# A hybrid SSD and gated-delta layer on one core: every engine's order taken from a list schedule over a first build

## The chip, the cores and the metric

The kernel runs on one core of a Trainium2 chip. The core has five engines that run their own instruction streams in order and wait for one another by semaphores: TensorE (PE in the profile, its weight loads PEld), VectorE (DVE), ScalarE (ACT), GpSimd (POOL) and SyncE (SP), which here issues nearly all DMA transfers. The metric is the device time of one execution in microseconds (us). The kernel before takes 2354.13 us in the median of three runs (2348.30 to 2360.07).

## The reference

One layer of width 2048 over 1024 latent tokens with a context of 256 tokens ahead of them:

```python
mod_lat = silu(c) @ w_ada + b_ada;  mod_ctx = silu(c_ctx) @ w_ada + b_ada      # shift, scale, gate
u_l = rms_norm(x, pre_w) * (1 + scale_l) + shift_l                             # u_c alike from ctx
z, xbc, dt, qkv, b, a = split_proj(u @ w_in)
xbc = silu(conv5(xbc) + bias);  qkv = silu(conv5(qkv))
y = ssd_scan in both directions (16 heads of 64, state 128, chunks of 128), the context's state first
o = gdn_scan in both directions (8 heads of 128, chunks of 128):
    v_new = u_i - w_i @ S;  o_i = q_i @ S + attn_i @ v_new;  S = S * dec + k_i^T @ v_new
    (u_i, w_i solve a unit triangular 128 x 128 system per chunk)
yo = concat(ssd_out_norm(y, z), gdn_out_norm(o, z))
out = x + gate_l * rms_norm(yo @ w_out, post_w)                                # latent tokens only
```

All is float32; the kernel makes each product of the large projections from two float16 parts of either factor (three matmuls per block).

## The kernel before, in words

Tokens stand in 10 chunks of 128 (8 latent, 2 context), channels on partitions. The program is one class, `Layer`; `build()` walks a list of steps. In order of time: `start` and the modulation (w_ada, w_in and x loaded; 0 to 200 us), `gates()` (step sizes and decays of all heads; its last vector result is `la`, L570, which L579 and L591 to L593 bring into the cumulative sums), the first GDN projections with `gate_rows()` (the gate's columns of w_ada in sixteen loads of 1 MB, three buffers `x`, matmuls L325), then eight GDN heads, four SSD quarters, and the output projection (L1138).

A GDN head `h` has these parts. `gdn_prep` makes for each chunk the product of k with itself (L693) and with q (L695), and the decayed matrices A (L697) with `gb`, whose decays come by DMA (L686). `invert_blocks` inverts the diagonal 32 x 32 blocks of all twenty matrices: four transposes (L715), a store to DRAM (L716, L717), a load of X (L721), and 30 times a pair of DVE operations, L726 and L728, each of which needs the one before. `gdn_chain` runs ten steps in each of two directions, d = 0 and 1; a step is PE L850 and L852 (state S with k and q), DVE L856 (r), PE L866 (r through the inverse), DVE L871 (xw) and ACT L873, PE L876, DVE L881 (the next S), PE L888, DVE L889 (o). Tile names carry the direction: `ps_c0`, `r1`, `S0`, `xw1`. `gdn_end` and `gdn_post` finish one head and start another. An SSD quarter runs over the ten chunks twice; in the second pass it reads the matrices E (two buffers, DMA).

Between these parts stand the projections of later blocks: `conv_block` and `z_block` load 512 KB of w_in at a time (six buffers `w`), split it in float16 parts (ACT L408 and L411, DVE L413, with a small sum on PE, L134), and `group` runs 48 matmuls (L437) into a PSUM bank; the bank is emptied by one ACT and four DVE operations (L498), and ACT L502 and DVE L503 follow. The banks are `ps_d` (two) and in the GDN heads `ps_e` (one). This is the work that fills PE while a chain waits. All order is set by the framework's own scheduler: each instruction has a priority by its place in the program, and the scheduler picks for each engine, by its own costs, the ready instruction with the best one. Semaphores are then set from the dependencies.

Of the kernel before, what the change touches and what calls it, by code (L numbers as in the profile page):

```python
# [1 line left out]

# [5 lines left out]
F32 = mybir.dt.float32  # L8
# [6 lines left out]
P = 128  # L15
DM = 2048
KB = DM // P
KH = KB // 2
NL = 1024
NC = 256  # L20
T = NL + NC
NCH = T // P
# [22 lines left out]
class Layer:  # L45


    def __init__(self, ctx, tc, a, out):
        self.ctx, self.tc, self.nc, self.a, self.out = ctx, tc, tc.nc, a, out
        self.pool = lambda name, bufs=1, **kw: ctx.enter_context(tc.tile_pool(name=name, bufs=bufs, **kw))  # L50
        self.const = self.pool("const")
        self.phase_pool = None
        self.psum = self.pool("psum", bufs=1, space=bass.MemoryType.PSUM)
        self.dram = self.pool("dram", space=bass.MemoryType.DRAM)
        self.sk = self.psum.tile([P, 512], F32, tag="s", name="ps_s", bufs=1)
        self.nd = self.nk = self.ns = 0
        self.z7 = [None, None]
# [1232 lines left out]
        self.phase_pool.close()  # L1290


@with_exitstack
def hybrid_layer_kernel(ctx, tc, a, out):
    Layer(ctx, tc, a, out).build()


_INS = ['x', 'c', 'ctx', 'c_ctx', 'w_ada', 'b_ada', 'pre_norm_w', 'post_norm_w', 'w_in', 'conv_ssd_w', 'conv_ssd_b',
        'conv_gdn_w', 'ssd_a_log', 'ssd_dt_bias', 'ssd_d', 'ssd_norm_w', 'gdn_a_log', 'gdn_dt_bias', 'gdn_norm_w',
        'w_out']  # L1300
# [19 lines left out]
```

## Time and profile before

| | before |
|---|---|
| median of 3 runs | 2354.13 us (2348.30 to 2360.07) |
| profiled execution, its own time | 2351.73 us |
| its span | 2350.0 us |
| PE busy | 2162.5 us, 92% |
| DVE busy | 1399.5 us, 60% |
| ACT busy | 998.5 us, 42% |
| mean granted clock of PE | 0.978 |

The span is the stretch from the first to the last instruction. An engine's busy time is the time in which it executed an instruction; time in which it waited for a semaphore is idle. In a table by stretches each row gives, for one stretch, the busy us of each engine with the number of instructions, then the granted clock of PE (1.00 is full speed), the busy share of the DMA engines, and GB/s. A wait reads: who waited, in which line and tile, for which engine's instruction, then the total, the number and the longest, in us. In a timeline a row is a start, a duration and an instruction (equal neighbours merged, with x and their number), and in brackets how long the engine had been idle and what released it.

### The profile page before, as it was taken

The numbers are of one execution on the slowest core, as the hardware profiler recorded it, in microseconds if no ns is written. First come the engines' busy times: TensorE is split into PE (matmuls) and PEld (weight loads), VectorE is DVE, ScalarE is ACT, GpSimd is POOL, SyncE is SP. The second block draws the span as 40 slices with busy tenths as digits, with TensorE's granted clock in tenths as the row PEclk, the third lists the DMA queues.
The fourth block names the chain that finished last, engine by engine and source line by source line (L and its number), as shares of the span: only waits on it lengthen the run. The fifth ranks groups of instructions, "written<-read, shape, count | busy, mean of one in ns | idle before, by whom it ended". The sixth has DMA issues, their size and how long they took to land. (4 is left out here: it accounts for less than half of the span.)

```text
span 2350.0 us, 41855 instructions
## 1 busy us (share of the span) xinstructions
PE 2162.5 (92%) x16070; PEld 1379.2 (59%) x16070; DVE 1399.5 (60%) x3499; ACT 998.5 (42%) x2493; POOL 268.7 (11%) x514
## 2 busy tenths in 40 slices
PE   4989999889999898998989999999999999899998
PEld 4334644456665655556555566555555555788887
DVE  5335543869694856858568486566767773511214
ACT  6026422344444352433524444465667584423320
POOL 1000001012111020111201110130303130000000
PEclk9999999999999999999999999999999999999999
DMA  9952347454444344343443444333465355212117
GB/s 323 348 164 55 80 145 217 117 131 106 134 115 120 101 126 116 88 133 93 121 119 85 127 123 115 99 90 108 111 183 149 98 164 195 68 37 73 55 37 269
DMA packets 397236, 301.71 MB, mean 128 GB/s; under 512 B 61339, under 2 KB 358684, under 8 KB 395628
## 3 DMA queue, kind: packets, MB, share of 16 engines
q1 hardware_dynamic: 386668, 293.80, 43.7%
q10 hardware_dynamic: 10368, 5.24, 0.8%
q8 instruction: 126, 2.06, 0.4%
q14 instruction: 74, 0.61, 0.1%
HBM read 241.41 MB, written 57.57 MB: 127 GB/s over the span
## 5 line engine op out<-in xcount | busy, mean ns | idle before, releaser
L437 PE MATMUL ps_d<-u,w 128*128 128x512 f16 (+1 forms) x4560 | 969.6, 357 | 8.3 <-DVE cv L498 4.6
L437 PEld LDWEIGHTS <-w 128*128 128x128 f16 x6048 | 595.3, 100 | 494.3 <-issue 36.4
L1138 PEld LDWEIGHTS <-u 128*128 128x128 f16 x3072 | 298.7, 98 | 50.9 <-DMA u<-in_w_out_dram 13.2
L437 PE MATMUL ps_e<-u,w 128*128 128x512 f16 (+1 forms) x1296 | 314.5, 376 | 0.0
L498 DVE SCALAR_TENSOR_TENSOR cv<-ps_d,taps,cv 128x496 f32<-128x496 f32 (+3 forms) x300 | 194.8, 650 | 80.0 <-ACT cv L492 38.6
L413 DVE SCALAR_TENSOR_TENSOR w<-w,scl 128x512 f16<-128x512 f32 (+1 forms) x204 | 149.9, 777 | 50.8 <-ACT w L411 50.3
L408 ACT ACTIVATE w<-w 128x1024 f16<-128x1024 f32 (+1 forms) x102 | 106.5, 1044 | 167.7 <-DMA w<-in_w_in_dram 101.5
L1138 PE MATMUL ps_d<-wx,u 128*128 128x256 f16 x1536 | 170.2, 273 | 4.6 <-DMA u<-in_w_out_dram 4.6
L1138 PE MATMUL ps_d<-w,u 128*128 128x256 f16 x1296 | 144.8, 273 | 5.7 <-DMA u<-in_w_out_dram 3.8
L1168 DVE SCALAR_TENSOR_TENSOR raw<-ps_d,inv,gp 128x256 f32<-128x256 f32 x59 | 28.4, 483 | 193.2 <-ACT jko L1166 193.2
L411 ACT ACTIVATE w<-w,scl 128x1024 f16<-128x1024 f32 (+1 forms) x102 | 112.3, 1133 | 36.2 <-DVE scl L145 16.5
L1166 ACT ACTIVATE jko<-ps_d,inv 128x256 f32<-128x256 f32 x59 | 27.8, 471 | 182.4 <-PE ps_d L1138 177.4
L989 ACT ACTIVATE E<-E,G 128x128 f32<-128x128 f32 x256 | 80.9, 388 | 35.1 <-DMA E<-gr 29.6
L690 ACT ACTIVATE gb<-gb 128x256 f32<-128x256 f32 x80 | 32.2, 413 | 147.0 <-DVE gb L676 144.0
L502 ACT ACTIVATE t<-cv 128x512 f32<-128x512 f32 (+1 forms) x98 | 55.7, 570 | 90.0 <-DVE cv L498 75.4
L676 DVE SCALAR_TENSOR_TENSOR gb<-gb,G,mneg 128x128 f32<-128x128 f32 x160 | 50.8, 345 | 69.2 <-DMA gb<-gr 67.9
L873 ACT ACTIVATE r<-ps_c,nb 128x128 f32<-128x128 f32 x128 | 45.7, 364 | 107.0 <-DVE xw L871 97.2
L876 PE MATMUL ps_c<-xw,vq 128*128 128x128 f32 x288 | 61.8, 304 | 30.8 <-DVE xw L871 14.2
L726 DVE TENSOR_TENSOR tp<-X 80x30 f32<-80x30 f32 (+14 forms) x240 | 77.6, 323 | 13.9 <-DMA X<-d 13.2
L876 PEld LDWEIGHTS ps_c<-xw,vq 128*128 128x128 f32 x288 | 47.4, 196 | 58.9 <-ACT r L873 33.7
L503 DVE SCALAR_TENSOR_TENSOR cv<-t,cv 128x512 f32<-128x512 f32 (+1 forms) x98 | 60.5, 618 | 31.7 <-ACT t L502 31.3
L728 DVE TENSOR_TENSOR X<-X,tp 80x30 f32<-80x30 f32 (+14 forms) x240 | 78.4, 327 | 0.6
(329 smaller groups left out, 3250.4 us busy)
## 6 DMA issues: line engine op xcount, KB each, us to landing
w<-in_w_in_dram SPq DMA_DIRECT2D x102, 512.0 KB
x<-in_w_ada_dram SPq DMA_DIRECT2D x48, 1024.0 KB
vq<-vq SPq DMA_DIRECT2D x128, 256.0 KB
E<-gr SPq DMA_DIRECT2D x64, 256.0 KB
u<-in_w_out_dram SPq DMA_DIRECT2D x24, 512.0 KB
gb<-gr SPq DMA_DIRECT2D x80, 128.0 KB
x<-in_x_dram SPq DMA_DIRECT2D x8, 1024.0 KB
vq<-gb SPq DMA_DIRECT2D x64, 128.0 KB
```

The costliest lines, as they stand in the source:

```text
L408: nc.scalar.activation(out=w16[h][:, 0], in_=w[h], func=AF.Square, accum_out=ssq[:, h:h + 1])
L411: nc.scalar.activation(out=w16[h][:, 0], in_=w[h], func=AF.Copy, scale=t)
L413: nc.vector.scalar_tensor_tensor(out=w16[h][:, 1, s], in0=w[h][:, s], scalar=t, in1=w16[h][:, 0, s], op0=ALU.mult, op1=ALU.subtract)
L437: self.nc.tensor.matmul(out=ps, lhsT=w16[k // KH][:, a, k % KH], rhs=self.u16[b][k][:, lo:lo + n], start=(k == 0 and i == 0), stop=(k == K ...
L498: nc.vector.scalar_tensor_tensor(out=o3[:, :, lo_o:hi_o], in0=p3[:, :, lo_o + s:hi_o + s], scalar=taps[tap], in1=o3[:, :, lo_o:hi_o], op0= ...
L502: nc.scalar.activation(out=t[:, 0:n], in_=o, func=AF.Tanh)
L503: nc.vector.scalar_tensor_tensor(out=o, in0=t[:, 0:n], scalar=1.0, in1=o, op0=ALU.add, op1=ALU.mult)
L726: nc.vector.tensor_tensor(out=t, in0=X[:, k + 1:, k:k + 1].to_broadcast(sh), in1=X[:, k:k + 1, 0:k].to_broadcast(sh), op=ALU.mult)
L728: nc.vector.tensor_tensor(out=X[:, k + 1:, 0:k], in0=X[:, k + 1:, 0:k], in1=t, op=ALU.add)
L876: nc.tensor.matmul(out=pS, lhsT=vq[:, 1], rhs=xw, start=True, stop=True)
L989: nc.scalar.activation(out=E[:, d, r], in_=E[:, d, r], func=AF.Identity, bias=self.G[:, j, c:c + 1])
L1138: self.nc.tensor.matmul(out=ps, lhsT=self.y16(k, p, s), rhs=w16[k // 4][:, q, k % 4], start=(i == 0 and j == 0), stop=(i == KB - 1 and j = ...
```

## The change

The kernel is built twice. The first build is the one before. From it the class `Plan` takes every instruction that the framework ordered, with its dependencies, buffers and priority, gives each a duration from tables by engine and size, and makes a list schedule: at each point the engine that is free earliest takes, of the instructions whose inputs are ready, the one with the best priority. Up to `fixed` = 250 us of planned time the program's own order is kept. A result reaches another engine 90 ns after its end (200 from PE), and a PE instruction is held to be ready another `lead` = 700 ns later; between dependent instructions of one engine the plan has no gap. A DMA starts 1300 ns after its issue and lands 500 ns after its last byte. Buffers count too: an instruction that reuses a place in SBUF or PSUM follows those that used it. The second build gets, for each engine, an edge from each instruction to the next of the plan (an order without a semaphore). No instruction's arithmetic changes; the second build gives its tiles to other buffers of the same pool in some places, and the number of semaphore instructions differs a little. Lines of the class stand two lower in the new file, so L866 is there L868.

```diff
+class Plan:
+    DVE_TT = ((1, 150), (128, 285), (256, 415), (512, 690))
...
+    AFTER = {"PE": 200, "SP": 0}
...
+        def issue(k, t):
+            nonlocal rate
+            e = self.engine[k]
+            free[e] = end = t + self.cost[k]
+            if self.dma[k]:
+                whole, alone = self.dma[k]
+                s = max(t + 1300, rate)
+                rate = s + max(whole, alone * .3)
+                end = s + max(whole, alone * .6) + 500
+            done[k] = True
+            if k < real:
+                self.order[e].append(self.names[k])
+            for q in after[k]:
+                gap = 0 if max(k, q) >= real or (e == self.engine[q] and not self.dma[k]) else self.AFTER.get(e, 90)
+                if gap and self.engine[q] == "PE":
+                    gap += self.lead
+                ready[q] = max(ready[q], end + gap)
+                count[q] -= 1
+                if not count[q]:
+                    heapq.heappush(will[self.engine[q]], (ready[q], self.prio[q], q))
...
+        while k < real and max(free.values()) < fixed:
...
+            issue(k, max(free[self.engine[k]], ready[k]))
+            k += 1
...
+        while not all(done):
+            best = None
+            for e in free:
+                while will[e] and will[e][0][0] <= free[e]:
+                    _, p, k = heapq.heappop(will[e])
+                    heapq.heappush(can[e], (p, k))
+                t = free[e] if can[e] else will[e][0][0] if will[e] else None
+                if t is not None and (best is None or t < best[0]):
+                    best = t, e
+            t, e = best
+            k = heapq.heappop(can[e])[-1] if can[e] else heapq.heappop(will[e])[-1]
+            issue(k, max(t, ready[k]))
...
+    def draw(self, tc, nc):
+
+        info = mybir.DependencyInfo(mybir.DependencyClass.NoSync, mybir.DependencyReason.SCHED_ONLY)
+        last = {b: a for names in self.order.values() for a, b in zip(names, names[1:])}
+        for i in nc.all_instructions():
+            if i.name in last:
+                tc.add_manual_dep(i, last[i.name], info, reason="order")
...
+    nc = build(Plan(*build(None), lead=700, fixed=250e3))[0]
```

Three places show how the order moves. The first is PE in a step of a GDN head's chain (`ps_c0_7506` and `ps_c1_7524` are the same step in the two directions; `ps_m_8344` and `ps_m_8358` hold transposes of a later head). Before:

```order
L850 MATMUL ps_c0_7506<-S0_7482,cv_4868 128x128
L852 MATMUL ps_c0_7506<-S0_7482,vq0_7484 128x128
L850 MATMUL ps_c1_7524<-S1_7500,cv_4868 128x128
L852 MATMUL ps_c1_7524<-S1_7500,vq1_7502 128x128
...
L866 MATMUL ps_c0_7506<-r0_7509,A_5681 128x128
...
L866 MATMUL ps_c1_7524<-r1_7527,A_5681 128x128
...
L876 MATMUL ps_c0_7506<-xw0_7514,vq0_7484 128x128
...
L888 MATMUL ps_c0_7506<-r0_7513,vq0_7484 128x128
L876 MATMUL ps_c1_7524<-xw1_7532,vq1_7502 128x128
```

Now:

```order
L852 MATMUL ps_c0_7506<-S0_7482,cv_4868 128x128
L854 MATMUL ps_c0_7506<-S0_7482,vq0_7484 128x128
...
L868 MATMUL ps_c0_7506<-r0_7509,A_5681 128x128
...
L852 MATMUL ps_c1_7524<-S1_7500,cv_4868 128x128
L854 MATMUL ps_c1_7524<-S1_7500,vq1_7502 128x128
...
L878 MATMUL ps_c0_7506<-xw0_7514,vq0_7484 128x128
...
L98 MATMUL ps_m_8344<-ident_138,cv_7808 128x128 x4
L98 MATMUL ps_m_8358<-ident_138,cv_7808 128x128 x4
L890 MATMUL ps_c0_7506<-r0_7513,vq0_7484 128x128
L868 MATMUL ps_c1_7524<-r1_7527,A_5681 128x128
```

The first gap holds three projection matmuls (L437) before, and the others three, one, three and none; now the gaps hold nine, one, six and sixty-one (L439), and the second direction's L868 comes after all of these.

The second place is DVE at the inversion of the next head's blocks (X_7346, tp_7347), about the same steps. Before:

```order
L726 TENSOR_TENSOR tp_7347<-X_7346 80x30
L881 SCALAR_TENSOR_TENSOR S0_7554<-S0_7518,cd_2200,ps_c0_7542 128x128
L728 TENSOR_TENSOR X_7346<-X_7346,tp_7347 80x30
L498 SCALAR_TENSOR_TENSOR cv_7808<-ps_d_7866,taps_7806,cv_7808 128x8x63
L726 TENSOR_TENSOR tp_7347<-X_7346 80x58
L889 TENSOR_TENSOR o_7413<-ps_c0_7542,o_7413 128x128
L728 TENSOR_TENSOR X_7346<-X_7346,tp_7347 80x29x2
L881 SCALAR_TENSOR_TENSOR S1_7572<-S1_7536,cd_2200,ps_c1_7560 128x128
L726 TENSOR_TENSOR tp_7347<-X_7346 80x84
L498 SCALAR_TENSOR_TENSOR cv_7808<-ps_d_7866,taps_7806,cv_7808 128x8x62
```

Now:

```order
L500 SCALAR_TENSOR_TENSOR cv_7808<-ps_d_7923,taps_7806,cv_7808 128x255
L873 TENSOR_SCALAR xw0_7514<-ps_c0_7506,pw_5483 128x128
L505 SCALAR_TENSOR_TENSOR cv_7808<-t_7920,cv_7808 128x512
L728 TENSOR_TENSOR tp_7347<-X_7346 80x30
L730 TENSOR_TENSOR X_7346<-X_7346,tp_7347 80x30
L728 TENSOR_TENSOR tp_7347<-X_7346 80x58
L730 TENSOR_TENSOR X_7346<-X_7346,tp_7347 80x29x2
...
L883 SCALAR_TENSOR_TENSOR S0_7518<-S0_7482,cd_2200,ps_c0_7506 128x128
L858 SCALAR_TENSOR_TENSOR r1_7527<-ps_c1_7524,eG_2197,vq1_7502 128x128
L500 SCALAR_TENSOR_TENSOR cv_7808<-ps_d_7923,taps_7806,cv_7808 128x255
```

Before, each of the sixty operations on X had an operation of the chain or of a projection behind it. Now the sixty stand together (56 of them left out here), and r1_7527, which the L868 above needs, comes after the last.

The third place is PE in the gates (`la` is their last vector result, `w_2225` the weights of a projection). Before:

```order
L134 MATMUL ps_s_63<-wsq_2227,ones_139 128x2
...
L437 MATMUL ps_d_2272<-u_165,w_2225 128x512
...
L437 MATMUL ps_d_2329<-u_165,w_2226 128x512
L579 MATMUL ps_m_2116<-mask_142,la_2111 48x128 x4
L579 MATMUL ps_m_2122<-mask_142,la_2111 48x128 x4
L579 MATMUL ps_m_2128<-mask_142,la_2111 48x128 x2
```

Now:

```order
L136 MATMUL ps_s_63<-wsq_2227,ones_139 128x2
...
L439 MATMUL ps_d_2272<-u_165,w_2225 128x512
...
L439 MATMUL ps_d_2329<-u_165,w_2225 128x512
L581 MATMUL ps_m_2116<-mask_142,la_2111 48x128 x4
L581 MATMUL ps_m_2122<-mask_142,la_2111 48x128 x4
L581 MATMUL ps_m_2128<-mask_142,la_2111 48x128 x2
```

Before, 92 projection matmuls stood between L134 and L579; now four stand between L136 and L581, the same two lines.

## Rows read from the trace of the kernel before

**Rows 1.** The page: the span, and busy us of PE (share, instructions)

```profile
span 2350.0 us, 41855 instructions
...
PE 2162.5 (92%) x16070; PEld 1379.2 (59%) x16070; DVE 1399.5 (60%) x3499; ACT 998.5 (42%) x2493; POOL 268.7 (11%) x514
```

**Rows 2.** Busy time by stretches, the columns as the first row says

```profile
core 0: us, PE busy (x) PEld busy (x) DVE busy (x) ACT busy (x) POOL busy (x), PEclk, DMA share, GB/s
...
400.00:500.00 100.00, 86.67 (x687) 45.75 (x686) 75.66 (x204) 43.63 (x107) 10.66 (x21) 0.95 0.44 112
500.00:1400.00 900.00, 833.76 (x6295) 526.53 (x6294) 635.45 (x1853) 356.96 (x954) 135.82 (x260) 0.97 0.44 116
...
1550.00:2000.00 450.00, 424.60 (x2480) 248.17 (x2478) 304.04 (x637) 293.69 (x794) 86.11 (x147) 0.99 0.49 141
```

**Rows 3.** Waits of PE, 500 to 1400 us (total, times, longest)

```profile
PE ps_c L888 <- DVE S L881: 14.4, 7, 3.3
PE ps_c L876 <- DVE xw L871: 14.2, 5, 3.2
PE ps_c L876 <- ACT r L873: 13.2, 7, 3.0
```

**Rows 4.** Waits of PE, 400 to 500 us

```profile
PE ps_m L693 <- DVE gb L700: 10.1, 4, 6.7
```

**Rows 5.** Busy time and clock around a pause that ended at 511.5 us

```profile
508.00:513.00 5.00, 1.73 (x7) 1.32 (x7) 2.46 (x9) 0.42 (x1) 0.00 (x0) 0.77 0.46 100
513.00:518.00 5.00, 5.00 (x18) 3.21 (x17) 2.23 (x9) 0.83 (x2) 0.00 (x0) 0.55 0.74 195
```

**Rows 6.** The page's groups of instructions: the block inversion on DVE

```profile
L726 DVE TENSOR_TENSOR tp<-X 80x30 f32<-80x30 f32 (+14 forms) x240 | 77.6, 323 | 13.9 <-DMA X<-d 13.2
...
L728 DVE TENSOR_TENSOR X<-X,tp 80x30 f32<-80x30 f32 (+14 forms) x240 | 78.4, 327 | 0.6
```

**Rows 7.** Timeline of DVE, 466 to 471 us (start, duration, instruction)

```profile
469.91 0.24 DVE L728 TENSOR_TENSOR X<-X,tp 80x84 f32<-80x84 f32 x1
470.19 0.22 DVE L726 TENSOR_TENSOR tp<-X 80x58 f32<-80x58 f32 x1
```

**Rows 8.** Timeline of all engines, 779 to 791 us, the inversion's input

```profile
779.61 0.43 SPq L717 DMA_DIRECT2D d<-ft  x1
...
783.94 1.06 SPq L721 DMA_DIRECT2D X<-d  x1
...
790.65 0.20 DVE L726 TENSOR_TENSOR tp<-X 80x30 f32<-80x30 f32 x1 [2.90 <-DMA X<-d]
```

**Rows 9.** Timeline of PE, 423 to 430 us, a run of products

```profile
423.52 6.85 PE L437 MATMUL ps_e<-u,w 128*128 128x512 f16 x31
```

**Rows 10.** Timeline of PE, 243 to 270 us, the gates

```profile
243.72 9.41 PE L437 MATMUL ps_d<-u,w 128*128 128x512 f16 x35 [2.84 <-ACT w L411]
...
253.11 12.46 PE L437 MATMUL ps_d<-u,w 128*128 128x512 f16 x57
265.88 4.57 PE L579 MATMUL ps_m<-mask,la 128*48 128x128 f32 x40 [0.31 <-DVE la L570]
```

**Rows 11.** Timeline of DVE, 244 to 254 us, the gates' polynomial

```profile
244.36 0.41 DVE L559 TENSOR_SCALAR s<-e 128x480 f32<-128x480 f32 x1
...
245.34 3.15 DVE L560 RECIPROCAL s<-s 128x480 f32<-128x480 f32 x1
...
249.54 0.75 DVE L413 SCALAR_TENSOR_TENSOR w<-w,scl 128x512 f16<-128x512 f32 x1
250.21 0.65 DVE L562 TENSOR_TENSOR s<-s 128x480 f32<-128x480 f32 x1
...
251.34 0.66 DVE L565 TENSOR_TENSOR p<-p,s 128x480 f32<-128x480 f32 x1
...
253.43 0.40 DVE L566 TENSOR_SCALAR p<-p 128x480 f32<-128x480 f32 x1
```

**Rows 12.** Busy time by stretches, the gate rows

```profile
340.00:350.00 10.00, 9.87 (x78) 3.42 (x76) 3.90 (x7) 1.30 (x2) 0.12 (x1) 1.00 1.09 348
```

More of the change, by code (lines that the diff above doesn't have):

```diff
@@ L1 @@
+import heapq
+import math
 from contextlib import ExitStack
@@ L1307, with build @@
     from concourse.bass_utils import run_bass_kernel_spmd as _run
-    nc = _bacc.Bacc("TRN2", target_bir_lowering=False, num_devices=1)
-    arrays, args = {}, {}
-    for name in _INS:
-        v = _np.ascontiguousarray(inputs[name])
-        arrays[f"in_{name}_dram"] = v
-        args[name] = nc.dram_tensor(f"in_{name}_dram", v.shape, mybir.dt.from_np(v.dtype), kind="ExternalInput").ap()
-    out = nc.dram_tensor("out_0_dram", (1, NL, DM), F32, kind="ExternalOutput").ap()
-    with _tile.TileContext(nc) as tc:
-        hybrid_layer_kernel(tc, args, out)
+    arrays = {f"in_{name}_dram": _np.ascontiguousarray(inputs[name]) for name in _INS}
+    def build(plan):
+        nc = _bacc.Bacc("TRN2", target_bir_lowering=False, num_devices=1)
+        args = {}
+        for name in _INS:
+            v = arrays[f"in_{name}_dram"]
+            args[name] = nc.dram_tensor(f"in_{name}_dram", v.shape, mybir.dt.from_np(v.dtype), kind="ExternalInput").ap()
+        out = nc.dram_tensor("out_0_dram", (1, NL, DM), F32, kind="ExternalOutput").ap()
+        with _tile.TileContext(nc) as tc:
+            hybrid_layer_kernel(tc, args, out)
+            ins = list(nc.all_instructions())
+            names, tiles = {i.name for i in ins}, list(tc.tiles)
+            bounds = {i.name: (i.op, [t.name for t in i.bass_pool_tiles or ()]) for i in ins
+                      if type(i).__name__ == "BassTilePoolBoundary"}
+            if plan is not None:
+                plan.draw(tc, nc)
+        return nc, tiles, bounds, names
+    nc = build(Plan(*build(None), lead=700, fixed=250e3))[0]
     r = _run(nc, [arrays], core_ids=[0])
```

127 lines of the change are left out of this document (added).

## The prediction

> **What bounds the kernel now.** I read the page first, then the busy time by stretches, then the waits of PE stretch by stretch, and last the timelines of the places where the order changes. TensorE is the bound: 2162.5 us busy of a span of 2350.0 [rows 1], so 187.5 us idle in the whole run, and the rest of what an order can win is the clock. The stretches place this [rows 2]: PE idles 13.3 us in 400–500, 66.2 in 500–1400 (heads 0 to 7 of the gated delta rule, GDN) and 25.4 in 1550–2000 (the four SSD quarters); 250–400 has almost none. The rest lies before 250 us and after 2000 us, where PE's order does not change (its first changed matmul is the 580th of 13111, at about 200 us; from about the 10100th on, the output projection, the order is again the same). In 500–1400 the waits are the chain of a head: L888 for S, L876 for xw and for r, some 14 us each [rows 3]. In 400–500 most is L693 waiting for gb [rows 4].
>
> The clock: after a pause of PE that ended at 511.5 us the granted clock was 0.77 in 508–513 and 0.55 in 513–518, against 1.00 when undisturbed [rows 5]: between its two levels, 1.2 and 2.4 GHz. Busy PE at half speed loses half its time: 5.00 x 0.45 = 2.25 us in the second of these rows and about 0.8 us in the first, so some 3.1 us for one fall. Over 500–1400 the granted clock is 0.97 [rows 2]: 3% of 833.8 us, about 25 us, lost. So 66 + 25 = 91 us is what an order could win there at most.
>
> **The change part by part.** It adds and removes no arithmetic; each engine has the same instructions before and after, so the sum is of waits alone. All durations come from the one profiled execution of 2351.73 us, whose span is 2350.0; it lies 2.4 us under the median of 2354.13, well inside the spread of the runs.
>
> 1. *The chain links in a head.* In the new order PE has more projection work between the matmuls of a chain (first order fence): by the orders, with 0.22 us for each 512-column product [rows 9], the work between L866 and L876 rises from 1.3 to 2.2 us in the median, from L876 to the next L850 from 1.8 to 3.2, from L866 to L888 from 2.1 to 4.1. A link needs about 1.3 us or more, so most of the 66 us [rows 2, 3] should go; I keep 14 us for the links that stay short, the DMA waits and the heads' ends.
>
> 2. *The block inversion on DVE.* Sixty dependent operations per head (L726, L728; X), which stood between other work, now stand side by side (second order fence). Their cost: 240 x 323 ns and 240 x 327 ns over eight heads [rows 6], so 156/8 = 19.5 us per head. Where two of them follow one another in the trace, the next one starts 0.28 us after the last for a duration of 0.24 [rows 7], so some 0.03 to 0.04 us more than the duration; sixty of these make 2 us, together 21.5 us in which DVE does nothing else. Everything that PE needs from DVE waits behind it: the chain's r and S, and the L498 that free the projection's PSUM banks. PE has work for the time by the order: in the head of the fences, from L866 of ps_c0 to L888 of the same tile, 68 products at 0.22 (15.0 [rows 9]), and eight transposes and three chain matmuls (an estimate of 1.6 together), some 16.6 us, against 0.6 (xw), 0.6 (L503), 21.5 and 0.4 (S): 23.1. Counted so, and with somewhat differing lead-ins, heads 1 to 6 leave PE idle for 8.9, 10.6, 6.5, 6.7, 6.5 and 6.7 us, 46 us together; heads 0 and 7 have enough work. Each such stall drops the clock once, 6 x 3.1 = 18 us [rows 5]. Then the block's input: from the issue of the transposed blocks' store at 779.61 to the issue of X's load at 783.94 and the end of the wait at 790.65 it took 11.0 us [rows 8]; in the new order 15 DVE instructions, one chain step, stand between the transposes and X. That is about as long as the 11 us; I take 1 us of wait per head, 6 us, with 0 and 5 per head as ends. So 500–1400 costs 14 + 46 + 18 + 6 = 84 us against 91: **-7 us**, with -40 (the stalls half covered and links free) and +25 (X late by 5 us) as ends.
>
> Beside other work it is otherwise: an operation of 0.75 us is followed by an independent one 0.67 us after its start [rows 11], while X's dependent ones keep 0.03 to 0.04 us beyond their duration [rows 7]. The Trainium skill (VectorE: DVE Perf Modes, section "The DRAIN you can't avoid") says that every DVE operation is followed by a flush of about its duration less 266 ns, and that the next one starts only when the pipe is empty. By that, X's operations of 325 ns in the mean would have some 0.06 us after each, 3.5 us a block in place of 2, an estimate; six stalls would be 9 us longer and the sum 2376. The rows differ (0.04 us behind an operation of 0.24, for which the page's figure gives nothing, and an overlap where nothing depends), so the sum keeps theirs.
>
> 3. *The gates.* The new order puts L579, which needs the gates' last result la, right after four projection matmuls (third order fence), where 92 of them (35 + 57) stood [rows 10]. DVE now runs the polynomial first, without the splits between. Its length by rows: L559 0.41, L560 3.15, six pairs of 0.66 + 0.40 [rows 11], and six more of 0.41 to 0.66 (3.7 together): 13.6 us. It starts at 242.2 (when the small operations ahead are done) to 244.4 (as before). So la is there at 255.8 to 258.0, while PE's four matmuls end about 244.8: 11 to 13 us idle, where before only 0.31 us was [rows 10]. With a part of a clock fall more than before: **+12 us** (9 to 16). PE's later work is not shortened by this, only moved.
>
> 4. *Gate rows.* Sixteen loads of 1 MB for L325 go through three buffers; while they ran, DMA moved 348 GB/s and PE was busy for 9.87 of 10 us [rows 12], about 3.0 us a load, with 3 to 18 projection matmuls between each pair of L325. The new order uses up that work early: the loads 5 to 10 get some 5 us of PE work each, and the last six groups of L325 follow one another without any. A load is issued only when its buffer is read, three groups earlier, so the last four loads start when the tenth group is read, and come 3 us apart: 4 x 3.0 less the 3 us of PE work there, about 9 us idle, and 1 us of clock: **+10 us** (0 if the loads keep ahead, 18 at most).
>
> 5. *The preparation of head 0.* Now projection work stands between the L693 that waited for gb; of 13.3 us idle [rows 2, 4] and some 2 of clock I take two thirds: **-10 us** (-15 to -4).
>
> 6. *From GDN to SSD.* 24 PE rows at the end of the last head stand without fill, with transposes that wait for POOL: **+4 us** (0 to 12).
>
> 7. *SSD quarters.* PE idles 25.4 us there [rows 2]. The new order gives five to nine products to each step of a quarter's first part and then has none for 18, 43 and 33 rows in the second parts of quarters 0, 1 and 2. What is won in the first part is lost in the second, since E's two buffers pace it: **+6 us**, with -15 (the waits of the first part gone, the second as now) and +25 as ends.
>
> Sum: -7 + 12 + 10 - 10 + 4 + 6 = +15, on 2351.7: **2367 us**.
>
> **The rivals.**
>
> *The waits go and the holes are covered: faster.* For it: 91 us stand in 500–1400 to be won, and the links get the work they lacked [rows 2, 3]. Against: the counts behind X in part 2. If PE's work covered X's block wholly, the 46 + 18 + 6 us would go and the time be 2297; if half, 2332. It decides from the point where PE has 23.1 us of work behind the last matmul that DVE needs.
>
> *Gains and holes cancel: no change.* Part 2 at -20 or the gates and gate rows at their lower ends (9 and 0) give 2351 to 2356.
>
> *X comes late: much slower.* One mechanism: DVE stands before X for its DMA, with the chain's r and S behind it. In the trace this happened once at 790.65, 2.90 us [rows 8], with other work around it. If the 11.0 us of store and load go past the work between by 5 us in each of seven heads, 35 us instead of 6 come on top: 2396, and with the SSD at its upper end 2415. It decides from the point where a chain step takes under 11 us.
>
> *Longer runs keep the clock: no change.* A row after a pause shows the clock at 0.55 [rows 5], and seven or eight such falls make the 25 us. The new order gathers PE's work in longer runs with fewer, longer pauses: six in 500–1400 by part 2. If these pauses brought no fall of the clock, its 18 us would not come: 2349. The Trainium skill (Perfetto Trace Analysis, section "Matmul Optimizations") says that TensorE scales its power with its use and asks for matmuls back to back in batches; the rows of before agree in that the fall follows a pause.
>
> **How the numbers follow.** A measurement of this kernel tells about 0.5% from no change, so 2342 to 2366 counts as the same. My forecast and its near neighbours above 2366: 0.36; X late: 0.10; cancelled, or no falls of the clock: 0.28; the holes covered: 0.26. So faster 0.26, same 0.28, slower 0.46. The range that holds the time 8 times in 10 is 2322 to 2408: below, to beyond the half-covered case; above, to X late with the rest as forecast. The forecast's own range is 2350 to 2385.
>
> **What would show it.** Right: in 500–1400 the waits L888 for S and L876 for xw and r shrink to a third, and six single PE pauses of 6 to 11 us appear, each ending with L866 or L888 behind r or S after the last L728; PE idle of 11 us or more before L579; about 9 us before the last L325; less than 5 us at L693. Wrong: X's sixty operations lie beside a busy PE, or 500–1400 falls by more than 30 us; or the pauses stand in SSD or past 2000 us, where I have almost none.

## The result and the profile after

The changed kernel is slower: 2416.04 us in the median (2408.59 to 2419.49) against 2355.22 (the kernel before, now with a fourth run), a ratio of 1.0256 (95% interval 1.0221 to 1.0292). I had forecast 2367, in a range up to 2408. The profiled execution has a span of 2406.9 us where the one before had 2350.0, so 56.9 more. Its page:

```profile
span 2406.9 us, 41756 instructions
...
PE 2157.6 (90%) x16070; PEld 1413.7 (59%) x16070; DVE 1440.6 (60%) x3499; ACT 1005.4 (42%) x2493; POOL 262.8 (11%) x514
```

PE idles 249.3 us instead of 187.5 [rows 1]. Its busy time is 4.9 us less, though the clock is lower. The busy time by stretches, columns as in [rows 2]:

```profile
400.00:500.00 100.00, 80.75 (x419) 39.65 (x411) 60.81 (x166) 28.82 (x80) 9.79 (x17) 0.89 0.41 113
500.00:1400.00 900.00, 817.28 (x6477) 530.41 (x6478) 654.58 (x1786) 366.58 (x977) 122.34 (x252) 0.95 0.43 115
1550.00:2000.00 450.00, 405.08 (x2319) 247.67 (x2318) 302.47 (x650) 290.66 (x803) 100.99 (x168) 0.93 0.45 125
```

The granted clock fell in all three (0.95, 0.97 and 0.99 before [rows 2]). The waits of PE over the whole run name the places:

```profile
PE ps_c L890 <- DVE S L883: 61.7, 8, 11.4
...
PE ps_y L1005 <- DVE E L998: 18.6, 9, 4.9
PE ps_m L327 <- DMA x<-in_w_ada_dram: 14.2, 4, 5.5
PE ps_m L581 <- DVE la L572: 11.7, 1, 11.7
...
PE ps_m L695 <- DVE gb L702: 7.3, 6, 1.8
PE ps_e L439 <- ACT w L413: 7.1, 1, 7.1
PE ps_c L852 <- DVE S L881: 7.0, 4, 1.8
...
PE ps_c L878 <- DVE xw L873: 1.2, 1, 1.2
...
PE ps_c L878 <- ACT r L875: 0.8, 2, 0.5
```

The chain links did as forecast: L876 for xw (now L878) had 14.2 us and has 1.2, and for r 13.2 [rows 3] and has 0.8. L693 for gb (now L695) went from 15.7 us in the whole run (10.1 of it in 400–500 [rows 4]) to 7.3. In their place stand L890 behind S, the wait behind the inversion, and three others: L327 for the gate rows' loads (no such wait before), L581 for la, L1005 for E (5.6 us before).

To see where the time went, I cut both runs at the same matmuls, with idle time and lost clock (busy time of PE times one less the granted clock) summed from windows of half a microsecond:

| stretch, ending at | length before, after | idle | clock lost |
|---|---|---|---|
| last matmul of the gates | 278.7, 271.3 | 54.4, 66.2 | 12.6, 13.0 |
| last matmul of the gate rows | 105.1, 145.3 | 0.6, 15.4 | 1.5, 7.3 |
| first L866 (head 0) | 110.8, 110.2 | 13.3, 11.3 | 1.9, 4.7 |
| last L866 (head 7) | 983.4, 1045.1 | 70.5, 86.8 | 22.1, 24.7 |
| first L962 (SSD) | 73.9, 25.1 | 1.5, 10.4 | 0.0, 5.0 |
| last L1003 | 395.8, 411.7 | 25.0, 30.9 | 5.1, 13.1 |
| end | 402.3, 398.2 | 22.1, 28.4 | 0.0, 3.8 |

Projection work is moved over some of these cuts (the fill of the last head, 73.9 against 25.1), so the lengths are to be added up: to the end of the gate rows +32.8, GDN from there to the first L962 +12.3, SSD +15.9, the rest -4.1.

One of the six pauses behind the inversion, on all engines; it is the place of the first two order fences:

```profile
688.41 0.38 PE L868 MATMUL ps_c<-r,A 128*128 128x128 f32 x2
...
688.63 9.01 PE L439 MATMUL ps_e<-u,w 128*128 128x512 f16 x41
690.30 0.20 DVE L728 TENSOR_TENSOR tp<-X 80x30 f32<-80x30 f32 x1 [3.72 <-DMA X<-d]
...
697.48 5.40 PE L439 MATMUL ps_d<-u,w 128*128 128x256 f16 x48
...
711.92 0.34 DVE L883 SCALAR_TENSOR_TENSOR S<-S,cd,ps_c 128x128 f32<-128x128 f32 x1
...
712.31 0.79 PE L890 MATMUL ps_c<-r,vq 128*128 128x128 f32 x2 [8.55 <-DVE S L883]
```

From the first of X's operations to the S behind the last one DVE needs 21.6 us; I had 21.5. PE's work ends at about 703.8 and L890 starts at 712.31. The first row of DVE shows that it waited 3.72 us for X's load. Over all heads that wait is 21.3 us; it was 13.2 before [rows 6]:

```profile
L728 DVE TENSOR_TENSOR tp<-X 80x30 f32<-80x30 f32 (+14 forms) x240 | 78.7, 328 | 29.3 <-DMA X<-d 21.3
```

The six pauses are 10.27, 8.55, 9.51, 10.21, 11.42 and 9.23 us, 59.2 together. After this one the clock stood at its lower level:

```profile
713.00:718.00 5.00, 4.45 (x17) 3.50 (x16) 4.80 (x12) 2.71 (x11) 0.00 (x0) 0.50 1.01 247
```

Behind the six, 1.7 to 4.3 us of clock were lost each, 18.5 together. A seventh pause, in head 0, hides under another name:

```profile
499.94 0.15 DVE L147 TENSOR_SCALAR scl<-hexp 128x1 int32<-128x1 int32 x1
...
500.22 2.17 ACT L413 ACTIVATE w<-w,scl 128x1024 f16<-128x1024 f32 x2
...
501.41 3.17 PE L439 MATMUL ps_e<-u,w 128*128 128x512 f16 x7 [7.09 <-ACT w L413]
```

DVE's small operation (L147) that gives the weights' scale stood behind X, so ACT could not make the float16 weights, and PE stood 7.09 us in L439.

The gates came as forecast (start, duration, instruction, idle time):

```profile
243.85 1.66 PE L439 MATMUL ps_d<-u,w 128*128 128x512 f16 x4 [3.32 <-ACT w L413]
257.18 6.08 PE L581 MATMUL ps_m<-mask,la 128*48 128x128 f32 x36 [11.66 <-DVE la L572]
```

### The profile page after: what moved, and what is told of

Same layout as the page of the kernel before. It is cut to its first block, busy times and chain, and to the rows that moved or that the text cites. A ratio compares the mean times of both kernels' runs of the same rounds, so it can differ in the third digit from the quotient of the medians.

```text
span 2406.9 us, 41756 instructions
## 1 busy us (share of the span) xinstructions
PE 2157.6 (90%) x16070; PEld 1413.7 (59%) x16070; DVE 1440.6 (60%) x3499; ACT 1005.4 (42%) x2493; POOL 262.8 (11%) x514
## 4 chain that ended last, share of the span: by engine, by line
PE 64%; DVE 16%; DMA 13%; ACT 2%; issue 2%; SPq 1%; POOL 1%; DVEq 0%; ACTq 0%; POOLq 0%
PE ps_d L439 25%; PE ps_d L1140 11%; PE ps_e L439 8%; DVE tp L728 3%; DVE X L730 3%; DMA gb<-gr 3%; DVE cv L500 2%; PE ps_m L327 2%; DMA d<-ft 2%; PE ps_m L439 2%; DMA vq<-gb 1%; PE ps_d L253 1%; DMA E<-gr 1%; DMA u<-in_w_out_dram 1%; DMA X<-d 1%
## 5 line engine op out<-in xcount | busy, mean ns | idle before, releaser
L439 PE MATMUL ps_d<-u,w 128*128 128x512 f16 (+1 forms) x4560 | 963.0, 356 | 7.2 <-DVE cv L500 3.4
L439 PEld LDWEIGHTS <-w 128*128 128x128 f16 x6048 | 596.4, 100 | 503.9 <-issue 33.7
L439 PE MATMUL ps_e<-u,w 128*128 128x512 f16 (+1 forms) x1296 | 313.6, 377 | 10.6 <-ACT w L413 7.1
L415 DVE SCALAR_TENSOR_TENSOR w<-w,scl 128x512 f16<-128x512 f32 (+1 forms) x204 | 144.6, 749 | 17.2 <-ACT w L413 16.5
L890 PE MATMUL ps_c<-r,vq 128*128 128x128 f32 x256 | 54.7, 297 | 62.8 <-DVE S L883 61.7
L728 DVE TENSOR_TENSOR tp<-X 80x30 f32<-80x30 f32 (+14 forms) x240 | 78.7, 328 | 29.3 <-DMA X<-d 21.3
L890 PEld LDWEIGHTS ps_c<-r,vq 128*128 128x128 f32 x256 | 47.2, 202 | 78.1 <-DVE S L883 65.7
L492 ACT ACTIVATE cv<-ps_d,taps 128x512 f32<-128x512 f32 (+1 forms) x44 | 27.2, 617 | 129.9 <-PE ps_d L439 128.9
```

The costliest lines, as they stand in the source:

```text
L415: nc.vector.scalar_tensor_tensor(out=w16[h][:, 1, s], in0=w[h][:, s], scalar=t, in1=w16[h][:, 0, s], op0=ALU.mult, op1=ALU.subtract)
L439: self.nc.tensor.matmul(out=ps, lhsT=w16[k // KH][:, a, k % KH], rhs=self.u16[b][k][:, lo:lo + n], start=(k == 0 and i == 0), stop=(k == K ...
L728: nc.vector.tensor_tensor(out=t, in0=X[:, k + 1:, k:k + 1].to_broadcast(sh), in1=X[:, k:k + 1, 0:k].to_broadcast(sh), op=ALU.mult)
L890: nc.tensor.matmul(out=po, lhsT=at, rhs=x, start=True, stop=True)
```

## The experiments

All ratios are to the kernel before on the same chip. An edit is told by its lines in `Plan` or where it is called; runs that mark a part of the program have line numbers three to five higher.

| run | ratio, interval |
|---|---|
| changed kernel | 1.0256 (1.0221 to 1.0292) |
| early_only | 1.0094 (1.0069 to 1.0119) |
| late_only | 1.0148 (1.0127 to 1.0170) |
| ssd_only | 1.0064 (1.0040 to 1.0089) |
| own_gap | 1.0043 (1.0021 to 1.0064) |
| own_late | 0.9941 (0.9922 to 0.9961) |
| own_mid | 0.9909 (0.9888 to 0.9931) |
| x_mid | 0.9875 (0.9853 to 0.9898) |
| store_swap | 1.0219 (1.0199 to 1.0238) |
| lead0 | 1.0471 (1.0449 to 1.0493) |
| own_mid_lead0 | 1.0199 (1.0175 to 1.0223) |
| own_mid_lead1400 | 0.9837 (0.9813 to 0.9861) |
| start_only | 1.0050 (1.0033 to 1.0067) |
| ssd_start | 1.0043 (1.0029 to 1.0057) |
| own_mid_start | 0.9691 (0.9667 to 0.9715) |
| mid_best | 0.9785 (0.9767 to 0.9803) |
| mid_best45 | 0.9996 (0.9985 to 1.0007) |

**Which part loses: early_only, late_only, ssd_only.** The order edges are drawn only for a part of the program; the rest is the framework's to order. The edit is that of late_only; `MARK` stands at the preparation of head 0. early_only has `if n in early`, and ssd_only draws the edges from the first SSD block on.

```diff
+        early = {i.name for i in list(nc.all_instructions())[:MARK[0]]}
-        last = {b: a for names in self.order.values() for a, b in zip(names, names[1:])}
+        last = {b: a for names in self.order.values() for p in [[n for n in names if n not in early]] for a, b in zip(p, p[1:])}
```

> Order edges only among instructions from the preparation of head 0 on (GDN, SSD, output); everything ahead of it (gates, gate rows) is left to the framework's scheduler as in the kernel before. Theory A (what is lost up to the last matmul of the gate rows, 33 us, is lost for good): 2416 - 33 = 2383. Rival B (the early holes are made up later, since the fill used there is only moved): 2410 to 2416. Rival C (PE's early order matters little and the plan's own start moves the later stages): above 2416.

> The complement: order edges only among the instructions up to the end of the gate rows; GDN, SSD and output are left to the framework's scheduler. Theory A: 2355 + 33 = 2388, with the GDN heads as in the kernel before (X interleaved, chain waits of some 40 us back). Rival B (early holes are made up later): 2355 to 2365.

> The changed kernel's plan, its order edges drawn only among the instructions from the first SSD block to the end; everything ahead of it is left to the framework's scheduler. Theory A (the SSD part of the plan loses by itself: waits for E of 4 to 5 us behind runs without fill and the clock): 15 us slower than the kernel before, ratio 1.006. Rival B (the SSD's loss is only the fill that the plan had used up in GDN): no slower than the kernel before.

Early alone costs 0.94% (22 us of 2355), late alone 1.48%, which is 25 us less than the changed kernel; 2.4 together against 2.56. So the parts add, and of the 33 us lost early 22 to 25 stay lost: late_only is nearer A than B (its ratio times 2355.22 is 2390), early_only about halfway between them (2377). SSD alone costs 0.64%, 15 us as A had it. By difference GDN costs some 20 us in the changed kernel.

**The inversion in one piece: own_gap, own_mid, own_late, x_mid.** A result of DVE counts as ready for the next DVE instruction 60 ns after its end, so that the plan puts other ready work between. In the changed kernel 472 of X's 480 operations follow another one of X directly; in the kernel before it was 37 and in own_gap 38. own_mid draws the edges in GDN only, own_late from head 0 to the end. In x_mid, drawn in GDN only, the 60 ns hold for X's operations alone.

```diff
-                gap = 0 if max(k, q) >= real or (e == self.engine[q] and not self.dma[k]) else self.AFTER.get(e, 90)
+                gap = 0 if max(k, q) >= real else (60 if e == "DVE" else 0) if e == self.engine[q] and not self.dma[k] else self.AFTER.get(e, 90)
```

> The plan with one number changed: a DVE result that the next DVE instruction needs counts as ready 60 ns after its end, not at once, so that the plan puts other ready work between (X's sixty operations and the gates' polynomial are interleaved again, 38 neighbours of 480 instead of 472, and 93 products stand before la instead of 4). Theory A (the six PE pauses behind X, 59 us, and the one before la, 12 us, come from DVE being held by one dependent chain): all seven go, with about 14 us of clock; 2416 - 85 = 2331, with the gate rows' waits (14 us and 6 of clock) left. Rival B (the pauses only show where PE's fill, moved forward into the chain links, is missing later): with DVE interleaved the links wait as in the kernel before, and the time ends at 2370 or above.

> The plan with the 60 ns between dependent DVE instructions, its order edges drawn only from the preparation of head 0 to the end of the last GDN head; gates, gate rows, SSD and output are left to the framework's scheduler. Theory A (with DVE interleaved the plan's order is a gain in GDN, and what was left over in the run with the 60 ns was lost in the gate rows and the SSD): in that run the stretch from the last gate-row matmul to the first L962 took 1136.0 us against 1168.1 before, so 32 us less than the kernel before, 2314 where that takes 2346 (ratio 0.986). Rival B (that stretch was shorter because its projection work had been done ahead or was left for later): within 8 us of the kernel before.

> As the last, but with order edges from the preparation of head 0 to the end of the program, SSD and output too. Theory A: the gain in GDN of 32 us less what the SSD quarters lose (17 us of clock and 14 of idle time more than before in the run with the 60 ns over the whole program, between the last L866 and the end, of which some 10 us is work moved): before less 10 to 15 us, ratio 0.995. Rival B: the loss in SSD was due to the early part; then the same as the run restricted to GDN.

> Order edges from the preparation of head 0 to the end of the last GDN head, as in the run at a ratio of 0.991, but with the 60 ns only where the waiting instruction is one of the inversion's sixty per head (41 neighbours of 480); all other dependent DVE instructions may follow at once, as in the changed kernel. Without any 60 ns this stretch would cost about 20 us (35 for everything from head 0 on less 15 for the SSD part), ratio 1.0085. Theory A (the seven PE pauses in GDN come from the inversion alone): the same as with the 60 ns everywhere, ratio 0.989 to 0.993. Rival B (it is the dependent pairs of DVE in general): half of the way or less, ratio 1.000 or above.

With the one number the whole program goes from 1.0256 to 1.0043, 50 us, not the 85 of theory A; its ratio times 2355.22 is 2365, nearer to B's 2370 than to A's 2331. All seven pauses of 7 to 11 us are gone, the one before la too (56.1 us idle up to the end of the gates). So they came from the order on DVE, as A says. But idle time between the first and the last L866 fell only from 86.8 to 60.4 us: 33 of the six pauses' 59.2 us came back there as other waits, which is B's part. The largest part is L695 for gb, 20.8 us there after 6.9 in the changed kernel:

```profile
PE ps_m L695 <- DVE gb L702: 21.3, 15, 3.1
```

(21.3 is for the whole run.) From head 0 on the same number makes 0.9941 of 1.0148 (own_late against late_only, 49 us); restricted to GDN the plan gains 0.9%, 21 us, somewhat less than A's 32. x_mid, at 0.9875, is no worse (the intervals overlap), so the inversion's operations are the ones that count, and not dependent DVE pairs in general (A). A run of GDN alone without the 60 ns was not made; its 1.0085 is a difference of two others.

**The gate rows: store_swap.** In the changed kernel the loads do not wait for a buffer. All engines, 386 to 409 us:

```profile
386.92 1.07 PE L327 MATMUL ps_m<-x,cw 128*32 128x256 f32 x16
...
390.35 0.25 SPq L345 DMA_DIRECT2D gate<-gt  x1
390.70 1.00 SPq L323 DMA_DIRECT2D x<-in_w_ada_dram  x2
...
395.83 1.94 PE L327 MATMUL ps_m<-x,cw 128*32 128x256 f32 x16 [5.47 <-DMA x<-in_w_ada_dram]
...
399.81 0.25 SPq L345 DMA_DIRECT2D gate<-gt  x1
...
400.16 0.99 SPq L323 DMA_DIRECT2D x<-in_w_ada_dram  x2
...
405.32 1.93 PE L327 MATMUL ps_m<-x,cw 128*32 128x256 f32 x16 [4.29 <-DMA x<-in_w_ada_dram]
```

SP issues two loads right after the store of a finished gate row (L345), and that store waits for PE's last L327 of a row. So a pair of loads starts only when the pair before has been used up, every 9.5 us, and DMA moves 210 GB/s in 390–410. In the kernel before the store stood one load later in SP's order.

```diff
...
+        for j in range(len(sp) - 2, -1, -1):
+            if sp[j] in gate and sp[j + 1] in self.loads:
+                sp[j], sp[j + 1] = sp[j + 1], sp[j]
```

> The changed kernel with one exchange on SP: each store of a finished gate row (the store that waits for PE's columns) goes behind the load of w_ada that follows it, which is the order of the kernel before. Theory A (the loads stand behind that store in SP's queue, so a pair of loads is issued only when the pair before is used up: 9.5 us a pair in place of 6): the three waits of 5.5, 4.3 and 4.3 us shrink to under 1.5 each, 2416 - 10 - 4 of clock = 2402. Rival B (there is no PE work left beside these loads, so they wait for the transfers in any order, 6 us a pair with 2.6 of PE work): waits of some 3 us each, 2410 or more.

After the exchange, on the same engines:

```profile
397.81 0.99 SPq L323 DMA_DIRECT2D x<-in_w_ada_dram  x2
...
400.34 5.08 SPq L323 DMA_DIRECT2D x<-in_w_ada_dram  x2
...
403.06 1.93 PE L327 MATMUL ps_m<-x,cw 128*32 128x256 f32 x16 [3.55 <-DMA x<-in_w_ada_dram]
...
406.05 1.93 PE L327 MATMUL ps_m<-x,cw 128*32 128x256 f32 x16 [1.05 <-DMA x<-in_w_ada_dram]
...
409.06 2.18 PE L327 MATMUL ps_m<-x,cw 128*32 128x256 f32 x16
...
411.98 1.07 PE L327 MATMUL ps_m<-x,cw 128*32 128x256 f32 x16 [0.74 <-DMA x<-in_w_ada_dram]
```

One of the two loads now stands ahead of the store, and the waits are 3.55, 1.05 and 0.74 us. Idle time in the gate rows falls from 15.4 to 6.8 us and lost clock from 7.3 to 5.3; the kernel goes from 1.0256 to 1.0219, 8.7 us. The two intervals overlap, so by the times alone the gain is not sure; the waits show it. That is theory A, a little short of its 14 us: 6.8 us stay, since PE has too little work beside the last loads, which is B's part.

**The lead: lead0, own_mid_lead0, own_mid_lead1400.**

```diff
-    nc = build(Plan(*build(None), lead=700, fixed=250e3))[0]
+    nc = build(Plan(*build(None), lead=0, fixed=250e3))[0]
```

> The changed kernel with lead = 0: the plan no longer holds a PE instruction back 700 ns behind its producers. Theory A (the lead is what spreads the chain links and takes away the waits of L876 and L888 of before, some 40 us and 20 us of waits too short to be seen): those waits come back in part, 20 to 40 us slower than the changed kernel, ratio to before 1.034 to 1.043. Rival B (the links are paid for by DVE and ACT queues, not by PE's place): within 8 us of the changed kernel, ratio 1.022 to 1.029.

> The run restricted to GDN with the 60 ns for every dependent DVE pair, and lead = 0. Theory A (the gain of 21 us comes from the lead, which gives each chain link more PE work and removes waits too short to be recorded as idle, 44 us before and 25 with the lead): without it the gain is gone, ratio 1.00 or above. Rival B (the lead mattered only behind the inversion, where the order without it has no fill at all): ratio 0.991 as with the lead.

> The same with lead = 1400. If more PE work per link goes on removing waits (theory A): 5 to 15 us less than with 700, ratio 0.985 to 0.989. If the fill then runs out at the heads' ends (theory B): ratio 0.993 or above.

Theory A in all three, and larger than expected: without the lead the changed kernel loses another 50 us, the run in GDN 68 us (0.9909 to 1.0199), and twice the lead gains 17. Waits of PE in lead0, 400 to 1560 us:

```profile
PE ps_c L852 <- DVE o L891: 36.5, 9, 18.7
PE ps_c L868 <- ACT o L865: 28.8, 7, 7.8
```

Not L876 and L888 come back but the links' first halves: PE goes right up to the next L850 or L866 (L852 and L868 here) and stands there, up to 18.7 us, behind the inversion. In own_mid_lead0, where X is spread, L876 for xw does come back, 16.0 us (14.2 before).

**The plan's DMA times: start_only, own_mid_start, ssd_start.** DVE had waited for X's load in seven heads, and PE in own_mid for gb, whose decays come by DMA:

```profile
PE ps_m L698 <- DVE gb L705: 22.5, 14, 3.7
PE ps_c L893 <- DVE S L886: 9.3, 7, 3.2
```

```diff
-                s = max(t + 1300, rate)
+                s = max(t + 3000, rate)
```

> The changed kernel with one number changed: 3000 in place of 1300 ns from a DMA's issue to its start in the plan; DVE's sixty stay together (472 neighbours). Theory A (two causes that add: the stalls behind the inversion stay, but DVE no longer waits for its input, 18.7 us in seven heads, and gb's and E's waits shrink): 20 to 45 us less than the changed kernel, ratio to before 1.007 to 1.017. Theory B (the belief about DMAs is the main cause, the inversion's stalls vanish with it): ratio below 1.00. Theory C (the stalls behind the inversion take up what is won): ratio 1.02 or above.

> The run restricted to GDN with the 60 ns, lead = 700, and 3000 in place of 1300 ns from a DMA's issue to its start in the plan. In the changed kernel DVE waited 2.2 to 4.6 us for the inversion's input in six heads, and in the run restricted to GDN PE waited 22.5 us for gb, whose decays come by DMA. Theory A (the plan holds DMAs too short): those waits shrink by half, 8 to 15 us less, ratio 0.985 to 0.988. Theory B (the loads are issued as late as their buffers allow, whatever the plan believes): ratio 0.989 to 0.993.

> Order edges only from the first SSD block on, with 3000 in place of 1300 ns; with 1300 this was 1.0064 of before, with 18 us of PE waits for E. Theory A (the plan takes E's loads for shorter than they are, so it leaves no PE work beside them): the loss shrinks to nothing, ratio 0.996 to 1.001. Theory B (the plan spends its PE work in a quarter's first part whatever the loads take): ratio 1.004 to 1.010.

This was the larger find. In the changed kernel the one number gives 1.0050 instead of 1.0256, 48 us, although X's operations still stand in one piece. start_only's waits of PE, 480 to 1600 us:

```profile
PE ps_c L852 <- DVE o L891: 22.5, 11, 5.3
PE ps_c L878 <- ACT r L875: 11.9, 5, 8.8
...
PE ps_c L890 <- DVE S L883: 3.6, 6, 1.2
```

The pauses behind X are now 5.30, 8.78, 3.36, 4.18 and 4.13 us, 25.8 in place of 66.3 with head 0's, and DVE waits 6.9 us for X's load in place of 21.3. Which loads the rest of the 48 us comes from was not taken apart. That is near theory A and a little beyond its range. In GDN with the 60 ns it gives 0.9691, 2283.06 us, more than A had hoped; the waits of PE from 380 to 1560 us:

```profile
PE ps_s L139 <- ACT w L413: 8.7, 4, 5.7
PE ps_d L442 <- DVE cv L503: 8.1, 3, 4.3
PE ps_c L893 <- DVE S L886: 6.8, 6, 1.9
```

The wait for gb is gone from the list's head, and idle time between the first and the last L866 falls from 64.1 to 28.7 us. In the SSD the wait for E, ssd_only first, then ssd_start:

```profile
PE ps_y L1008 <- DVE E L1001: 16.1, 9, 4.1
```

```profile
PE ps_y L1008 <- DVE E L1001: 6.6, 5, 3.1
```

It shrinks by 9.5 us, but the time only from 1.0064 to 1.0043, within B's range, and the two intervals overlap: idle time after the first L1138 rose to 34.6 us (27.0 in ssd_only). What else the SSD part loses stays open.

**Together: mid_best, mid_best45.** The three gains in one (the 60 ns for X alone, lead 1400, 3000 or 4500 ns for a DMA).

> Order edges only in GDN, with the three numbers that gained one by one: 60 ns before each of the inversion's operations alone, lead = 1400, 3000 ns to a DMA's start. If the gains add (0.9 to 0.4% for the first, 0.7% for the second, 2.2% for the third, on 0.991): ratio 0.958 to 0.963. If the waits that they remove are the same ones: 0.966 to 0.971.

> As the last with 4500 ns to a DMA's start. If the plan's DMAs are still too short at 3000: 5 us or more less than the last run. If 3000 was enough, or fill runs out: the same or slower.

mid_best, at 0.9785, is in neither range and worse than own_mid_start alone. mid_best45, at 0.9996, is slower again, as its second case allows, but by 50 us. The gains do not add up, and why stays open. X's operations in one piece do not explain it: 123 of them follow another one directly in mid_best, 73 in the slower mid_best45 and 52 in own_mid_start, and in neither of the two does a PE pause over 2 us stand behind them. Which of the numbers spoils it was not tried. The best version is own_mid_start, the plan in GDN only with 60 ns and 3000 ns: 2283.06 us, 3.1% faster than before and 5.5% faster than the change.

## Why the prediction was wrong

The direction and most of the places were right, the size was not: the sum was +15 us and the profile shows +57. In idle time and lost clock the sum missed by 75 us, of which 33 did not show in the time (the last section): 26 between the first and the last L866 (points 1 and 2), 11 in the gate rows, 11 in the preparation of head 0, 10 between GDN and SSD, 8 in the SSD and 10 after it. Point by point:

1. *Links.* I kept 14 us of waits. Of the 86.8 us idle between the first and last L866, 59.2 are the six pauses, so 27.6 were left. Against that stands a gain that I had not seen (the last section).
2. *The inversion.* The block's length (21.5, measured 21.6) and the heads of the six pauses were right, and the clock too (18 us; 18.5 behind the six pauses, 24.7 in all there). **The step that failed most is the next one: "I take 1 us of wait per head" for X's load, and "heads 0 and 7 have enough work".** DVE waited 18.7 us in heads 1 to 7, 2.7 each, and head 0 stood too, by way of the weights' scale: 66.3 us of pauses where I had 52 (46 and 6). In the head shown above the DVE work between the transposes and X was over some 4 us before the load had landed; I had taken it for as long as the 11.0 us of store and load.

The step rested on a misread row. I wrote that X came late once before, 2.90 us; [rows 6] have 13.2 us of it, in five heads (1.94, 2.90, 1.57, 3.74 and 3.08). In each of the five PE stood at L888 for the S that was behind X on DVE, as here beside the 790.65 of [rows 8]:

```profile
791.16 0.80 PE L888 MATMUL ps_c<-r,vq 128*128 128x128 f32 x2 [2.47 <-DVE S L881]
```

These five pauses are 10.9 of the 14.4 us of L888 in [rows 3], which I had read as links short of work: the late load was already the larger part of that wait. Behind the step lay also a cause that I had read in the diff and not followed: the plan starts a DMA 1300 ns after its issue, where the trace had 6.7 us from X's issue to its use [rows 8]. The same number sets where the fill goes for every load of a head, and by start_only it is worth 48 us in the whole program, as much as the inversion's order (own_late against late_only, 49 us; the two overlap, since both take away the same pauses).

3. *Gates.* 11 to 13 us idle forecast, 11.66 measured.
4. *Gate rows.* +10 forecast; idle and clock say +21. I had the loads wait for their buffers. They waited for a store ahead of them in SP's queue: I had gone through PE's order there and not through SP's. store_swap gives 8.7 us back.
5. *Head 0.* -10 forecast. gb's waits shrank, but idle and lost clock together went from 15.2 to 16.0 us, with head 0's pause in L439 in their place.
6. *From GDN to SSD.* +4 forecast, +9 idle and +5 of clock measured.
7. *SSD.* +6 forecast; +15 by ssd_only. The waits for E are where I had put them (18.6 us), the clock was not in my sum: 8 us more lost. After the last L1003, where I had almost nothing, idle time is 6 us and lost clock 3.8 us higher.

Of the rivals the third, X late, came closest: 2396 by its price. Its mechanism is there, a chain step being shorter than the load, but its 5 us a head were 2.7, so that its time is near is in part luck: terms that I had too small elsewhere made up the rest. I gave it 0.10, and it was not another case but part of the likeliest one. The fourth, that longer runs keep the clock, is out: all six pauses brought a fall. My errors in 2, 4, 5, 6 and 7 all go one way, since each was an estimate of a wait in the new order by the rows of the old; a range that lets them cancel was too narrow. The sixty operations of X, of 0.328 us in the mean, took 21.6 us, which is 0.03 us beyond each duration. The Trainium skill (VectorE: DVE Perf Modes, section "The DRAIN you can't avoid") gives a flush of about the duration less 266 ns, by an estimate some 0.06 us here; the measurement decides against that size.

## What to carry to other kernels

A list schedule that takes its DMA transfers for too short puts work where its input has not landed, and an in-order queue makes everything behind it wait; one number there was worth 2% of this kernel. A long run of dependent operations on an engine that also feeds others must be spread on purpose, since a greedy plan sees no cost in keeping it together. When an order is judged, go through every queue that it moves, the DMA issuing one too, and test it part by part: in GDN this plan, with two of its numbers changed, is a gain of 3%, while its parts ahead of GDN and in the SSD lost wherever they were tried alone. And before a wait is read as a lack of work, follow it one step further: the engine that was waited for may have been waiting itself, here for a DMA.

## What the runs showed of the hardware that I had not expected

PE's busy time hides waits. The kernel before, then the changed one, five products each followed by a chain matmul, no idle time in the record:

```profile
947.26 1.24 PE L437 MATMUL ps_d<-u,w 128*128 128x512 f16 x5
948.44 0.49 PE L876 MATMUL ps_c<-xw,vq 128*128 128x128 f32 x2
```

```profile
663.56 1.24 PE L439 MATMUL ps_e<-u,w 128*128 128x512 f16 x5
664.64 0.38 PE L868 MATMUL ps_c<-r,A 128*128 128x128 f32 x2
```

The five take 1.18 us to the next start before and 1.08 after, at full clock in both; the recorded 1.24 covers the difference, since a matmul's record is 0.38 us long and products start 0.217 apart. In the whole run the same 16070 matmuls take 33 us less after than before, when lost clock is taken off the busy time: 2162.5 - 43.1 = 2119.4 us before, 2157.6 - 71.7 = 2085.9 after. This is why the changed kernel loses 90 us more in idle time and clock (61.8 and 28.6) and is only 57 us longer; own_mid in the same way gains 20 us with 5 us less idle time. Starts that came late without idle time are part of it: those at full clock that are more than 0.02 us later than the median of their kind make some 37 us from the gate rows to the first L962 before, 23 in the changed kernel and 30 in own_mid. This sum depends on what is counted as late (own_mid_lead0's expectation has 44 and 25 by another count), and that these are waits for semaphores is inferred from the starts; no run showed it by itself.
